# First mixer of a two-layer decoder trunk: 12 query projections in place of 16, rotary rows placed by transfers, and one reciprocal for two tiles

## The chip, the cores and the metric

The kernel runs on one core of one Trainium2 chip. The metric is the device time of one execution, in microseconds (us); a kernel's time is the median of several runs. The kernel before takes 1875.57 us (median of 3 runs, 1875.18 to 1875.59). Engines are named as in the profile: PE is the matmul engine and PEld its weight loads, DVE the vector engine, ACT the scalar engine, POOL the GpSimd engine, and SP the engine that issues most of the transfers.

## The reference

The input is 512 tokens of 1024 numbers. Two layers each do half a gated FFN, a token mixer, and half a gated FFN, all with residual sums and root-mean-square norms. The first layer's mixer is multi-head latent attention with 16 heads, the second layer's is a sparse attention. Only the first mixer's form is rewritten. It computes:

```python
proj = h @ w_in
c_q, c_kv, k_rope = proj[..., :384], proj[..., 384:640], proj[..., 640:]
q = (rmsnorm(c_q, q_norm) @ w_uq).reshape(B, S, 16, 64 + 32)
kv = (rmsnorm(c_kv, kv_norm) @ w_ukv).reshape(B, S, 16, 64 + 64)
q_nope, q_rope = q[..., :64], apply_rotary(q[..., 64:], cos, sin)   # 32 rotary numbers a head
k_rope = apply_rotary(k_rope, cos, sin)                             # one for all heads
s = (q_nope . k_nope + q_rope . k_rope) * 96 ** -0.5                # causal
p = softmax(s);  o = p @ v;  return o @ w_o
```

`apply_rotary` takes a vector's two halves x1, x2 and gives x1 cos - x2 sin, x1 sin + x2 cos.

## The kernel before

All products run in a form that splits each fp32 operand into a high part (a copy by ACT) and a low part (the difference, by DVE or POOL), and does three matmuls for each product: high by high, high by low, low by high (`mm3`, lines 166 to 168; `split`, line 170). Weights come by a transfer into a raw tile `wr` of two buffers, ACT copies the high part and DVE, or POOL while `lo_pool` is set, subtracts the low part (`wslab`, line 136).

The mixer (`mla`, line 664) holds everything transposed: a row is a feature, 512 tokens lie along it. It projects the input with six weight slabs of 128 features (`pc` and `pr` on PE, tiles of 128x512), three for the query latent `cqh`/`cql`, two for the key-value latent, and one for the rotary key. A head then has one query tile of 128 rows: 64 plain rows, 32 rotary rows and the same 32 rotary rows with their halves swapped. `query` (line 771) therefore does one projection for each head, 9 matmuls of 128x512 (three parts of the latent by three products), multiplies it on DVE by a table `cst` that has ones, cosines and sines, and splits it (high on ACT, low on POOL for all but the first two heads). The key tile of a head has 64 plain rows and 64 rotary rows, so that one score product adds plain and rotary parts. `keys` (line 762) projects two heads at a time, 6 matmuls, and splits each half of the result straight into the 64 rows of that head's key tile: two copies on ACT and two differences on DVE for a pair. `vals` (line 745) makes the values, half of the heads at a time.

The attention is a list of 64 tiles, 16 heads `h` by four query blocks `i` = 3, 2, 1, 0, with 512, 384, 256 and 128 keys (`attend`, line 591). `front` (line 781) does a tile's scores `s` on PE, the shift and row minimum on DVE (`softmax_tile`, line 657, shown as CUSTOM_DVE at line 661), the exponential with its row sum on ACT, a reciprocal of the sum on DVE (line 791) and the product with it on POOL (line 792). Four tiles later `probs_T` (line 611) transposes the tile on PE (`pt`), and ACT and DVE split it into `pth` and `ptl`. `end` (line 795) does the head's product with the values on PE (`o`, line 627). The scores have two banks, so PE cannot put a third tile of scores down before DVE has read the first of the three.

In between, where the order of the program has room, PE works on what later heads need: `query(h + 2)` at the start of each head, `keys` for a pair two heads ahead, the second half of the values, and from head 8 on parts of the output projection `po` (`w_o`, line 637). A scheduler puts the instructions of each engine into one fixed order; at run time each engine takes its own in that order and waits for semaphores of the others. SP takes its transfers in order too.

The sparse mixer uses the same `softmax_tile`, and one reciprocal for each branch of a tile (`probs` in `nsa`).

Of the kernel before, what the change touches and what calls it, by code (L numbers as in the profile page):

```python
# [55 lines left out]
NG = 3  # L56

# [7 lines left out]
class Kern:  # L65
# [13 lines left out]
    def setup(self):  # L79
# [8 lines left out]
        self.sts, self.nst = [small[:, 12 + 3 * i : 15 + 3 * i] for i in range(6)], 0  # L88
# [563 lines left out]
    def stat(self):  # L652

        self.nst += 1
        return self.sts[self.nst % 6]
# [8 lines left out]
    def mla(self, gain_next):  # L664
        nc, tc, a = self.nc, self.tc, self.a
        with ExitStack() as pools:
# [4 lines left out]
            cst = mp.tile([P, S], F32, name="cst")  # L671
            nc.scalar.dma_start(cst, a["c_rope"])
            mask = mp.tile([P, S], F32, name="mask")
# [3 lines left out]
            kh, kl = self.parts(self.four()), self.parts(self.four())  # L677
            ckvp, self.qt = self.parts(self.four()), self.parts(self.four())
# [10 lines left out]
            def rows(col):  # L689
                pb = self.norm_bcast(col)  # L690
                t = tp.tile([P, S], F32, tag="o", bufs=12, name="row")
                nc.scalar.activation(t, pb, AF.Copy)
                return t
# [21 lines left out]
            for k in range(2):  # L715
                c = tp.tile([P, S], F32, tag="o", bufs=12, name="c")
# [6 lines left out]
            p = self.proj(a["mla_w_in"][5], P, xh, xl, "pr")  # L723
            kr = tp.tile([P, S], F32, tag="o", bufs=12, name="kr")
            nc.vector.tensor_tensor(kr, p, row, op=ALU.mult)
            crot = tp.tile([P, S], F32, tag="p", bufs=6, name="crot")
            nc.scalar.dma_start(crot, a["c_krope"])
            nc.vector.tensor_tensor(kr, kr, crot, op=ALU.mult)
            kr2 = tp.tile([64, S], F32, tag="ot", bufs=1, name="kr2")
            nc.scalar.activation(kr2, kr[64:128, :], AF.Copy)  # L730
            krs = tp.tile([P, S], F32, tag="o", bufs=12, name="krs")
            nc.vector.tensor_tensor(krs[64:128, :], kr[0:64, :], kr2, op=ALU.add)
            up = slice(64, 128)
            self.split(krs[up, :], kh[0][up, :], kl[0][up, :])

            def rotary(i):
                nc.scalar.activation(kh[i][up, :], krs[up, :], AF.Copy)
                nc.gpsimd.tensor_scalar(kl[i][up, :], f32v(kl[0][up, :]), 1.0, 1.0, op0=ALU.mult, op1=ALU.mult)

            rotary(1)  # L740


            vt = [[None] * 4 for _ in range(4)]

# [23 lines left out]
            def query_slab(h):  # L768
                return self.wslab(a["mla_w_q"][h], (3, P), "act")

            def query(h, w=None):
                p = self.proj(None, P, cqh, cql, "pq", w or query_slab(h))
                t = tp.tile([P, S], F32, tag="tq", bufs=2, name="tq")
                nc.vector.tensor_tensor(t, p, cst, op=ALU.mult)
# [4 lines left out]
            qs, oh, ol, o32 = {}, [], [], [None]  # L779

            def front(h, i):
                if i == 3 and 2 < h + 2 < H:
                    qs[h + 2] = query(h + 2)
# [5 lines left out]
                st = self.stat()  # L789
                self.softmax_tile(s, mask[:, S - n : S], i, nq[:, i : i + 1], p_sb, st[:, 0:1], st[:, 1:2])  # L790
                nc.vector.reciprocal(st[:, 2:3], st[:, 1:2])
                nc.gpsimd.tensor_scalar(p_sb[:, :n], p_sb[:, :n], st[:, 2:3], 1.0, op0=ALU.mult, op1=ALU.mult)
                return p_sb, last

            def end(h):
                o = self.bank("o", "o")
                self.pv(o, pth[h % 2], ptl[h % 2], lambda j: vt[j][h // 4][:, h % 4, :], True, True)
                if h % 2 == 0:
                    o32[0] = tp.tile([P, S], F32, tag="o32", bufs=2, name="o32")
                self.o_out(o, o32[0], h % 2, tp)  # L800
                if h % 2 == 1:
                    hi = tp.tile([P, S], F32R, tag="o", bufs=12, name="oh")
                    lo = tp.tile([P, S], F32R, tag="o", bufs=12, name="ol")
# [6 lines left out]
                if h % 2 == 1 and h + 3 < H:  # L810
                    keys((h + 3) // 2)
                if h >= 8 and h % 2 == 0:
                    self.w_o(a["mla_w_o"][0], oh[:4], ol[:4], [h // 2 - 4], False)
# [7 lines left out]
            cq = self.norm_col(QL, sums[1], eps=eps)  # L821
            nc.vector.tensor_scalar(nq, cq, -MLA_SCALE, None, op0=ALU.mult)
            for i in range(2, 4):
# [535 lines left out]
```

## Time and profile before

| what | us |
|---|---|
| median of 3 runs | 1875.57 |
| the profiled execution, own time | 1875.46 |
| its span, first to last instruction | 1873.7 |
| PE busy in the span | 1852.1 |
| first mixer: projections (344 to 396) | 52 |
| first mixer: attention with what lies between (396 to 530) | 134 |
| first mixer: rest of the output projection (530 to 558) | 28 |
| sparse mixer's attention (1301 to 1510) | 209 |

Lines are those of the kernel before. An engine's busy time counts overlapping instructions once. Matmuls overlap, so a matmul of 389 ns does not cost PE 389 ns: what it costs is the distance from its start to the next one's. A wait is shown in square brackets behind an instruction, with the engine that ended it.

### The profile page before, as it was taken

The numbers are of one execution on the slowest core, as the hardware profiler recorded it, in microseconds if no ns is written. First come the engines' busy times: TensorE is split into PE (matmuls) and PEld (weight loads), VectorE is DVE, ScalarE is ACT, GpSimd is POOL, SyncE is SP. The second block draws the span as 40 slices with busy tenths as digits, with TensorE's granted clock in tenths as the row PEclk, the third lists the DMA queues.
The fourth block names the chain that finished last, engine by engine and source line by source line (L and its number), as shares of the span: only waits on it lengthen the run. The fifth ranks groups of instructions, "written<-read, shape, count | busy, mean of one in ns | idle before, by whom it ended". The sixth has DMA issues, their size and how long they took to land.

```text
span 1873.7 us, 32771 instructions
## 1 busy us (share of the span) xinstructions
PE 1852.1 (99%) x12460; PEld 1687.8 (90%) x12460; DVE 1546.0 (83%) x2920; ACT 1080.7 (58%) x2039; POOL 241.9 (13%) x331
## 2 busy tenths in 40 slices
PE   8999999999999999999999999999999999999998
PEld 8999999878889999998999999988888889999997
DVE  8988886588789988886998888665988989988885
ACT  8545554478766544554655454435887866454454
POOL 0000000046710000000000000014666500000000
PEclk9999999999999999999999999999999999999999
DMA  6333332111232333322333333223122133333321
GB/s 244 128 102 102 102 107 98 56 50 46 71 120 94 120 104 104 102 93 93 108 113 103 112 112 98 97 93 103 63 72 65 35 110 124 111 104 102 106 79 67
DMA packets 75902, 183.26 MB, mean 98 GB/s; under 512 B 9040, under 2 KB 37072, under 8 KB 75744
## 3 DMA queue, kind: packets, MB, share of 16 engines
q1 hardware_dynamic: 72800, 176.39, 28.7%
q10 hardware_dynamic: 2944, 4.77, 0.7%
q8 instruction: 98, 1.61, 0.3%
q14 instruction: 60, 0.49, 0.1%
HBM read 178.96 MB, written 2.16 MB: 97 GB/s over the span
## 4 chain that ended last, share of the span: by engine, by line
PE 51%; DVE 2%; ACT 0%; issue 0%; DMA 0%; POOL 0%; ACTq 0%; DVEq 0%; SPq 0%
PE pd L166 4%; PE pd L168 4%; PE pd L167 4%; PE px L361 3%; PE px L362 3%; PE px L363 3%; PE pg L361 2%; PE pg L363 2%; PE pg L362 2%; PE pq L362 2%; PE pq L361 2%; PE pq L363 2%; PE o L1163 2%; PE pt L1138 2%; PE pp L166 1%; PE pp L168 1%
## 5 line engine op out<-in xcount | busy, mean ns | idle before, releaser
L167 PE MATMUL pd<-al,wd 128*128 128x512 f32 x576 | 224.1, 389 | 0.0
L168 PE MATMUL pd<-ah,wd 128*128 128x512 f32 x576 | 224.0, 389 | 0.0
L166 PE MATMUL pd<-ah,wd 128*128 128x512 f32 x576 | 224.0, 389 | 0.0
L361 PE MATMUL px<-four,wh 128*128 128x256 f32 x632 | 175.3, 277 | 0.3 <-ACT pg L493 0.2
L362 PE MATMUL px<-four,wh 128*128 128x256 f32 x632 | 174.5, 276 | 0.0
L363 PE MATMUL px<-four,wl 128*128 128x256 f32 x632 | 174.5, 276 | 0.0
L362 PE MATMUL pq<-four,wh 128*128 128x256 f32 x632 | 174.5, 276 | 0.0
L363 PE MATMUL pq<-four,wl 128*128 128x256 f32 x632 | 174.4, 276 | 0.0
L361 PE MATMUL pq<-four,wh 128*128 128x256 f32 x632 | 174.4, 276 | 0.0
L174 ACT ACTIVATE wd<-wdr 128x384 fp32r<-128x384 f32 x192 | 99.3, 519 | 102.0 <-issue 76.9
L175 DVE TENSOR_TENSOR wl<-s,wh 128x512 fp32r<-128x512 f32 x79 | 54.5, 690 | 119.7 <-ACT wh L174 119.7
L413 DVE SCALAR_TENSOR_TENSOR h<-pd,h 128x512 f32<-128x512 f32 x216 | 147.5, 683 | 6.1 <-PE pd L168 6.1
L168 PEld LDWEIGHTS pd<-ah,wd 128*128 128x128 f32 x576 | 108.1, 188 | 22.5
L174 ACT ACTIVATE wh<-s 128x512 fp32r<-128x512 f32 x79 | 49.8, 630 | 134.5 <-PE px L362 128.8
L166 PEld LDWEIGHTS pd<-ah,wd 128*128 128x128 f32 x576 | 108.1, 188 | 19.5
L167 PEld LDWEIGHTS pd<-al,wd 128*128 128x128 f32 x576 | 108.0, 188 | 19.5
L147 ACT ACTIVATE w<-wr 128x1024 fp32r<-128x1024 f32 (+5 forms) x91 | 80.3, 890 | 75.0 <-PE po L168 17.5
L361 PEld LDWEIGHTS px<-four,wh 128*128 128x128 f32 x632 | 118.6, 188 | 1.2 <-ACT pg L493 0.9
L362 PEld LDWEIGHTS px<-four,wh 128*128 128x128 f32 x632 | 118.7, 188 | 0.0
L361 PEld LDWEIGHTS pq<-four,wh 128*128 128x128 f32 x632 | 118.6, 188 | 0.0
L363 PEld LDWEIGHTS px<-four,wl 128*128 128x128 f32 x632 | 118.6, 188 | 0.0
L362 PEld LDWEIGHTS pq<-four,wh 128*128 128x128 f32 x632 | 118.6, 188 | 0.0
(362 smaller groups left out, 6102.0 us busy)
## 6 DMA issues: line engine op xcount, KB each, us to landing
wr<-in_w_gu SPq DMA_DIRECT2D x93, 512.0 KB, 3.2
ru<-in_w_gu SPq DMA_DIRECT2D x79, 512.0 KB, 4.2
wdr<-in_w_down SPq DMA_DIRECT2D x192, 192.0 KB, 2.4
wdr<-in_w_down SPq DMA_DIRECT2D x24, 256.0 KB, 2.9
wr<-in_mla_w_o SPq DMA_DIRECT2D x8, 512.0 KB, 3.2
wr<-in_nsa_w_q SPq DMA_DIRECT2D x8, 512.0 KB, 3.2
th<-btab_d SPq DMA_DIRECT2D x16, 256.0 KB, 3.3
wr<-in_nsa_w_o SPq DMA_DIRECT2D x8, 512.0 KB, 3.4
```

What stands on the lines that cost most here:

```text
L147: self.copied = nc.scalar.activation(wh[:, m], raw[:, m], AF.Copy)
L166: mm(out, wh, xh, start=first, stop=False)
L167: mm(out, wh, xl, start=False, stop=False)
L168: return mm(out, wl, xh, start=False, stop=last)
L174: nc.scalar.activation(hi, src, AF.Copy)
L175: (nc.gpsimd if pool else nc.vector).tensor_tensor(lo, src, f32v(hi), op=ALU.subtract)
L361: mm(out, wh[:, p], xh, start=first and p == 0, stop=False, skip_group_check=True)
L362: mm(out, wh[:, p], xl, start=False, stop=False, skip_group_check=True)
L363: mm(out, wl[:, p], xh, start=False, stop=last and p == KP - 1, skip_group_check=True)
L413: nc.vector.scalar_tensor_tensor(self.h[c], p, 0.5, self.h[c], op0=ALU.mult, op1=ALU.add)
L1138: nc.tensor.transpose(pt[:, j * P : j * P + P], p_sb[:, j * P : j * P + P], self.ident)
L1163: mm(out, vs[g][:, j, br * P : (br + 1) * P], x, start=False, stop=last and t == 1 and j == 2 * z + 1, skip_group_check=True)
```

## The change

Queries. The weight columns are laid out anew: eight slabs hold the 64 plain columns of two heads each, and four slabs hold the 32 rotary columns of four heads each. `queries(pair)` does one projection for the plain rows of two heads, `turned(f)` one for the rotary rows of four heads. `turned` multiplies its result by two tables `rot` (cosines and sines) on DVE and splits both products into a tile `qr`. `queries` splits a pair's result in one operation on all 128 rows (ACT, then DVE) into a tile `wide`, and transfers, issued by SP, put the plain 64 rows and twice 32 rotary rows into each head's tile; only the first pair is split straight into place. Swapped halves are no longer projected for queries: the keys' rows for the sines are swapped instead (the order of `kr` in `mla_w_in` and the signs in `c_krope`).

Keys. `keys` also splits a pair in one operation into another `wide` tile and four transfers place it; only the first pair goes straight into place. The rotary rows of the other three key tiles are placed by six transfers instead of copies.

Order. The rotary key, the first rotary projection and the first pair of queries come ahead of the keys and values. `lo_pool` is set before the rotary key's projection, so the low parts of its weights and of those after it are made by POOL. An exponential of one column is put in the code ahead of the first values. `keys` is called in `front` and `w_o` at heads 10 to 13 (`OUT`) instead of behind heads 8, 10, 12 and 14.

Reciprocals. Two tiles of a head share one reciprocal of two columns, and POOL's two products come behind it. In the sparse mixer the two branches of a short tile share one.

```diff
+OUT = 10, 11, 12, 13
...
-            def query(h, w=None):
-                p = self.proj(None, P, cqh, cql, "pq", w or query_slab(h))
-                t = tp.tile([P, S], F32, tag="tq", bufs=2, name="tq")
-                nc.vector.tensor_tensor(t, p, cst, op=ALU.mult)
-                qh, ql = self.qtile(), self.qtile()
-                self.split(t, qh, ql, pool=h > 1)
-                return qh, ql
...
             def keys(pair, w=None):
                 p = self.proj(a["mla_w_k"][pair], P, ckvh, ckvl, "pk", w)
+                t = wide[0]
+                if pair:
+                    self.split(p, t[:, :S], t[:, S:])
                 for e in range(2):
-                    b = (2 * pair + e) % 4
-                    self.split(p[64 * e : 64 * e + 64, :], kh[b][0:64, :], kl[b][0:64, :])
+                    x, m = (2 * pair + e) % 4 * S, slice(64 * e, 64 * e + 64)
+                    if not pair:
+                        self.split(p[m, :], kh[e][m, :], kl[e][m, :])
+                        continue
+                    for z in range(2):
+                        nc.sync.dma_start(f32v(k4[z])[m, x : x + S], f32v(t)[m, z * S : z * S + S])
...
+            def turned(f, w=None):
+                p = self.proj(None, P, cqh, cql, "pq", w or query_slab(H // 2 + f))
+                for z in range(2):
+                    t = f32v(wide[1])[:, z * S : z * S + S]
+                    nc.vector.tensor_tensor(t, p, rot[z], op=ALU.mult)
+                    x = 2 * z * S
+                    self.split(t, qr[:, x : x + S], qr[:, x + S : x + 2 * S], pool=f > 0)
+            def queries(pair, w=None):
+                p = self.proj(None, P, cqh, cql, "pq", w or query_slab(pair))
+                t = wide[1]
+                if pair:
+                    self.split(p, t[:, :S], t[:, S:])
+                for e in range(2):
+                    q, m, o, j = sets[2 * (pair % 2) + e], slice(64 * e, 64 * e + 64), 64 - 64 * e, 32 * ((2 * pair + e) % 4)
+                    if pair:
+                        nc.sync.dma_start(f32v(q)[m, :], f32v(t)[m, :])
+                    else:
+                        self.split(p[m, :], q[m, :S], q[m, S:])
+                    for z in range(2):
+                        nc.sync.dma_start(f32v(q)[o + 32 * z : o + 32 * z + 32, :], f32v(qr)[j : j + 32, 2 * z * S : 2 * z * S + 2 * S])
...
             def front(h, i):
-                if i == 3 and 2 < h + 2 < H:
-                    qs[h + 2] = query(h + 2)
+                if i == 3 and h % 2 == 0 and h + 2 < H:
+                    queries(h // 2 + 1)
+                if i == 1 and h % 2 == 0 and 2 <= h < H - 2:
+                    keys(h // 2 + 1)
+                if i == 3 and h % 4 == 1 and h + 3 < H:
+                    turned((h + 3) // 4)
+                if i == 3 and h in OUT:
+                    self.w_o(a["mla_w_o"][0], oh[:4], ol[:4], [OUT.index(h)], False)
...
-                nc.vector.reciprocal(st[:, 2:3], st[:, 1:2])
-                nc.gpsimd.tensor_scalar(p_sb[:, :n], p_sb[:, :n], st[:, 2:3], 1.0, op0=ALU.mult, op1=ALU.mult)
+                some.append((p_sb[:, :n], st[:, 4 + x : 5 + x]))
+                if x % 2:
+                    nc.vector.reciprocal(st[:, 3 + x : 5 + x], st[:, 3 + x : 5 + x])
+                    for t, r in some:
+                        nc.gpsimd.tensor_scalar(t, t, r, 1.0, op0=ALU.mult, op1=ALU.mult)
+                    some.clear()
...
+            turned(0)
+            queries(0)
...
             for pair in range(2):
                 keys(pair, [t[:, pair] for t in w])
-            wv = self.wslab(a["mla_w_v"][0], (2, S))
-            wq = query_slab(0)
-            vals(0, wv)
...
-            for i in range(2, 4):
-                rotary(i)
-            for h in range(3):
-                qs[h] = query(h, wq if h == 0 else None)
+            nc.scalar.activation(self.tiny[:, 1:2], self.tiny[:, 0:1], AF.Exp)
+            vals(0)
```

In the changed kernel lines count one higher up to line 663 (line 166 before is line 167), and more behind it. Three places show how instructions move.

On PE, where the second head (head 1) begins, the kernel before has query projections between the scores `s` and the transposes `pt`:

```order
L166 MATMUL pq<-cqh_4264,w 128x512
L167 MATMUL pq<-cql_4265,w 128x512
L168 MATMUL pq<-cqh_4264,w 128x512
L166 MATMUL s<-four,q 128x512
L167 MATMUL s<-four,q 128x512
L168 MATMUL s<-four 128x512
L166 MATMUL s<-four,q 128x384
L167 MATMUL s<-four,q 128x384
L168 MATMUL s<-four 128x384
L166 MATMUL pq<-cqh_4159,w 128x512
L167 MATMUL pq<-cql_4160,w 128x512
L616 MATMUL pt<-ident,p 128x128 x4
```

On PE at the same place the changed kernel has:

```order
L169 MATMUL pq<-cqh_4270,w 128x512
L167 MATMUL s<-four 128x512
L168 MATMUL s<-four 128x512
L169 MATMUL s<-four 128x512
L167 MATMUL s<-four 128x384
L168 MATMUL s<-four 128x384
L169 MATMUL s<-four 128x384
L617 MATMUL pt<-ident,p 128x128 x7
L167 MATMUL s<-four 128x256
L168 MATMUL s<-four 128x256
L169 MATMUL s<-four 128x256
L617 MATMUL pt<-ident,p 128x128 x2
```

The projections between them are gone: this head, and the one after it, consist of scores, transposes and the product with the values alone.

On SP the kernel before has, from the second half of the values on, only weight loads (`wr<-in_...`):

```order
L144 DMA wr<-in_mla_w_v 128x1024
L144 DMA wr<-in_mla_w_q 128x384
L144 DMA wr<-in_mla_w_k 128x256
L144 DMA wr<-in_mla_w_q 128x384 x2
L144 DMA wr<-in_mla_w_k 128x256
L144 DMA wr<-in_mla_w_q 128x384 x2
```

On SP in the changed kernel the same loads stand behind transfers from `qr` and `wide` into the query tiles (`four`, `q_4037`) and key tiles (`four`):

```order
L145 DMA wr<-in_mla_w_v 128x1024
L788 DMA four<-qr 32x1024 x3
L784 DMA four<-wide_4039 64x1024 x2
L788 DMA four<-qr 32x1024
L145 DMA wr<-in_mla_w_k 128x256
L145 DMA wr<-in_mla_w_q 128x384
L788 DMA q_4037<-qr 32x1024 x3
L761 DMA four<-wide_4038 64x512 x4
L788 DMA q_4037<-qr 32x1024
L784 DMA q_4037<-wide_4039 64x1024 x2
L145 DMA wr<-in_mla_w_k 128x256
L145 DMA wr<-in_mla_w_q 128x384 x2
```

Each pair of heads now has ten transfers ahead of and between its weight loads, and some of them wait for heads that still read the tile they write.

On ACT, in the first FFN, far ahead of the mixer, the kernel before has the copies of the products:

```order
L477 ACTIVATE gains<-pg,gains 128x1 x2
L493 ACTIVATE pg<-px 128x256
L477 ACTIVATE gains<-pg,gains 128x1
L495 ACTIVATE uq<-pq 128x256
L497 ACTIVATE uq<-px 128x256
L174 ACTIVATE ah<-tu 128x512
```

On ACT at that place the changed kernel has:

```order
L494 ACTIVATE pg<-px 128x256
L478 ACTIVATE gains<-pg,gains 128x1
L858 ACT_TABLE_LOAD
L858 ACTIVATE gains<-gains 128x1
L496 ACTIVATE uq<-pq 128x256
L498 ACTIVATE uq<-px 128x256
L175 ACTIVATE ah<-tu 128x512
L501 ACTIVATE pg<-px 128x256
```

The exponential of one column depends on nothing in the mixer and has moved into the first FFN, with a load of its table; the FFN's own table is loaded again after eight more instructions, and the mixer's first exponential still has its own load.

More of the change, by code (lines that the diff above doesn't have):

```diff
@@ L87, in setup @@
         self.vtc, self.small_sums, self.stc = small[:, :12], small[:, 12:16], small[:, 32:]
-        self.sts, self.nst = [small[:, 12 + 3 * i : 15 + 3 * i] for i in range(6)], 0
+        self.sts, self.nst = [small[:, 12 + 4 * i : 16 + 4 * i] for i in range(5)], 0
         self.gains = cp.tile([P, 64], F32, name="gains")
@@ L670, in mla @@
             self.scr = tp, "p", 6
-            cst = mp.tile([P, S], F32, name="cst")
-            nc.scalar.dma_start(cst, a["c_rope"])
-            mask = mp.tile([P, S], F32, name="mask")
+            rot = [self.xp.tile([P, S], F32, tag="w2", bufs=2, name="rot"), mp.tile([P, S], F32, name="rot")]
+            for z in range(2):
+                nc.scalar.dma_start(rot[z], a["c_rope"][z])
+            qr = mp.tile([P, 4 * S], F32R, name="qr")
+            q2 = mp.tile([P, 4 * S], F32R, name="q2")
+            wide = [mp.tile([P, 2 * S], F32R, name=f"wide{z}") for z in range(2)]
+            mask = self.xp.tile([P, S], F32, tag="w2", bufs=2, name="mask")
             nc.scalar.dma_start(mask, a["c_mask"])
@@ L676, in mla @@
             ptl = [mp.tile([P, 3 * PTS + S], F32R, name=f"ptl{i}") for i in range(2)]
-            kh, kl = self.parts(self.four()), self.parts(self.four())
-            ckvp, self.qt = self.parts(self.four()), self.parts(self.four())
+            k4 = [self.four(), self.four()]
+            kh, kl = self.parts(k4[0]), self.parts(k4[1])
+            ckvp, q1 = self.parts(self.four()), self.four()
+            sets = [t[:, x * S : x * S + 2 * S] for t in (q1, q2) for x in (0, 2)]
             xh, xl = self.xh, self.xl
@@ L690, in rows @@
                 pb = self.norm_bcast(col)
-                t = tp.tile([P, S], F32, tag="o", bufs=12, name="row")
+                t = tp.tile([P, S], F32, tag="o", bufs=10, name="row")
                 nc.scalar.activation(t, pb, AF.Copy)
@@ L715, in mla @@
             for k in range(2):
[L716 removed]
+                c = tp.tile([P, S], F32, tag="o", bufs=10, name="c")
                 nc.vector.tensor_tensor(c, ps[k], rkv, op=ALU.mult)
@@ L721, in mla @@
                 ckvl.append(lo)
[L723 to L740, printed above, removed]
             vt = [[None] * 4 for _ in range(4)]
+            qs, oh, ol, o32, some = {}, [], [], [None], []
             def vals(half, w=None):
@@ new lines, in queries @@
+            def queries(pair, w=None):
[9 more added lines that the diff above has]
+                        self.split(p[m, :], q[m, :S], q[m, S:])
+                    for z in range(2):
+                        nc.sync.dma_start(f32v(q)[o + 32 * z : o + 32 * z + 32, :], f32v(qr)[j : j + 32, 2 * z * S : 2 * z * S + 2 * S])
+                    qs[2 * pair + e] = q[:, :S], q[:, S:]
@@ L1128, in front2 @@
                 p_sb = tp.tile([P, S], F32, tag="p", bufs=6, name="p")
-                for br in range(2):
-                    bs = slice(br * m, br * m + m)
-                    probs(h, br, i, sb[:, bs], p_sb[:, bs])
+                probs(h, (0, 1), i, sb, p_sb)
                 return p_sb, last
```

69 lines of the change are left out of this document (42 added, 27 removed).

## The prediction

> **What bounds the kernel now.** First the page's busy times:
>
> ```profile
> span 1873.7 us, 32771 instructions
> PE 1852.1 (99%) x12460; PEld 1687.8 (90%) x12460; DVE 1546.0 (83%) x2920; ACT 1080.7 (58%) x2039; POOL 241.9 (13%) x331
> ```
>
> PE is busy for 99% of the span. That is an average, so I read the stages next, by windows (stretch, its length, then busy time of PE, PEld, DVE, ACT, POOL):
>
> ```profile
> 344.00:396.00 52.00, 52.00 (x250) 43.50 (x250) 31.20 (x74) 23.98 (x43) 3.26 (x5) 1.00 0.19 60
> 396.00:530.00 134.00, 129.89 (x727) 110.07 (x726) 106.07 (x319) 104.72 (x271) 87.11 (x112) 1.00 0.18 58
> ...
> 396.40:411.40 15.00, 13.23 (x74) 10.57 (x73) 12.42 (x45) 13.02 (x32) 12.02 (x16) 1.00 0.20 62
> ...
> 520.10:527.90 7.80, 7.37 (x50) 6.31 (x48) 7.51 (x25) 6.75 (x18) 2.13 (x4) 1.00 0.20 67
> ...
> 1301.00:1510.00 209.00, 207.59 (x1192) 174.47 (x1190) 187.06 (x596) 172.88 (x436) 132.38 (x164) 1.00 0.19 62
> ```
>
> In the mixer's projections PE never waits. In its attention PE is idle for 4.1 of 134 us, of which 1.77 lie in the first 15 us. DVE is busy 79% there and ACT 78%. So a matmul taken out of this stage shortens the kernel by its slot, as long as PE stays the engine that is last. The stretch from 520.10 is the exception to learn from: the last two heads, with hardly any projection between their scores. There DVE is busy for 96% of the time, and PE waits for it.
>
> **What a slot is worth.** The time line of PE, first and last of 22 matmuls of 128x512 that follow each other:
>
> ```profile
> 515.11 0.39 PE L168 MATMUL po<-oh,w 128*128 128x512 f32 x1
> ...
> 519.87 0.39 PE L168 MATMUL po<-oh,w 128*128 128x512 f32 x1
> ```
>
> 21 distances in 4.76 us are 0.2267 us for one matmul of 128x512. The Trainium skill's page "TensorE: Matmul & The Clock Gate" (section "Wait — 56ns, not 53.3ns?") gives 215.7 ns from start to start at 512 columns; the trace has 226.7 at a granted clock of 1.00, so the measured one counts, and by the page's figure the first term below would be 7.8 us in place of 8.2.
>
> **Term 1, the projections.** What writes and reads `pq` in the mixer:
>
> ```profile
> L166 PE MATMUL pq<-cqh,w x48: 387/397/478, 390.2 to 504.1; 128*128 128x512 f32 x48
> ...
> L167 PE MATMUL pq<-cql,w x48: 387/391/397, 390.5 to 504.4; 128*128 128x512 f32 x48
> ...
> L168 PE MATMUL pq<-cqh,w x48: 388/393/478, 390.7 to 504.6; 128*128 128x512 f32 x48
> L774 DVE TENSOR_TENSOR tq<-pq,cst x16: 671/680/692, 393.0 to 505.0; 128x512 f32<-128x512 f32 x16
> ```
>
> 144 matmuls are 16 projections of 9. Twelve projections are 108. **36 x 0.2267 = 8.16 us less.** No other matmul is added or removed.
>
> **Term 2, the start of the attention.** PE's two longest waits there:
>
> ```profile
> 397.51 0.44 PE L166 MATMUL s<-four 128*128 128x384 f32 x1 [0.25 <-DVE tq L774]
> ...
> 400.24 0.39 PE L166 MATMUL s<-four 128*128 128x256 f32 x1 [1.01 <-DVE small L661]
> ```
>
> Scores wait because DVE still works on the norm's column and on the queries of heads 0 to 2. In the changed order the norm's column and the queries of heads 0 and 1 come ahead of the first values, whose 24 matmuls (5.4 us) cover them. All 1.77 us could go, or none if another wait takes the place; I take **1.3 us less**.
>
> **Term 3, heads without projections.** Fewer projections, done for two or four heads at once, leave heads with scores, transposes and values alone. By the order these are heads 1, 2, 4, 7, 13, 14 and 15, seven against two before (14 and 15). What such a head costs is seen in the stretch of 96% DVE, whose scores begin at:
>
> ```profile
> 520.09 0.28 PE L166 MATMUL s<-four 128*128 128x256 f32 x1
> ...
> 520.58 0.31 PE L166 MATMUL s<-four 128*128 128x128 f32 x1
> ...
> 521.44 0.50 PE L166 MATMUL s<-four 128*128 128x512 f32 x1 [0.19 <-DVE small L661]
> ...
> 523.33 0.44 PE L166 MATMUL s<-four 128*128 128x384 f32 x1
> ...
> 524.87 0.33 PE L166 MATMUL s<-four 128*128 128x256 f32 x1
> ...
> 525.73 0.22 PE L166 MATMUL s<-four 128*128 128x128 f32 x1
> ```
>
> These are 2 + 1 + 4 + 3 + 2 + 1 = 13 blocks of 128 keys, and a head has 10. PE is idle for 7.80 - 7.37 = 0.43 us, so 0.33 us a head. DVE's softmax step gives the upper end (mean 543 ns):
>
> ```profile
> L661 DVE CUSTOM_DVE_ANT_0 p<-s,mask,small 128x512 f32<-128x512 f32 (+1 forms) x64 | 34.0, 543 | 3.8 <-PE s L168 2.5 <-PE pt L616 0.4 <-POOL w L153 0.2
> ```
>
> If PE loses one more such step in each of these heads, it is 0.33 + 0.54 = 0.87 us. I take 0.5, nearer to the row that was seen: five more heads give **2.5 us more**, with ends of 1.6 and 4.4. What speaks against the upper end is that DVE itself gets less to do in the attention:
>
> ```profile
> L791 DVE RECIPROCAL small<-small 128x1 f32<-128x1 f32 x64 | 10.0, 158 | 6.3 <-ACT p L662 5.3
> L175 DVE TENSOR_TENSOR four<-pk,four 64x512 fp32r<-64x512 f32 x16 | 11.0, 687 | 3.4 <-ACT four L174 3.3
> ```
>
> 32 reciprocals go (5.1 us), key differences fall from 16 to 9 (4.8), products with the rotary table from 16 to 8 (5.4), and query differences on DVE rise from 2 to 11 (6.2): about 9 us less, all beside PE's work except in the bare heads. The shared reciprocal also makes a tile wait for its neighbour's exponential, some 0.6 us; the four tiles between scores and transposes hide it while POOL and DVE are not behind.
>
> **Term 4, transfers and weights.** No transfer within the chip is in the trace of before. The nearest are small loads (KB each, us to landing) and the issue of one on SP:
>
> ```profile
> wr<-in_mla_w_q SPq DMA_DIRECT2D x16, 192.0 KB, 2.3
> ...
> cb<-btab_d SPq DMA_DIRECT2D x16, 64.0 KB, 2.7
> ...
> wr<-in_mla_w_k SPq DMA_DIRECT2D x6, 128.0 KB, 2.0
> ...
> 402.38 0.33 SPq L144 DMA_DIRECT2D wr<-in_mla_w_k  x1
> ```
>
> The tightest place is the keys of heads 4 and 5. From the end of `pk` to the scores of head 4 it takes a copy on ACT (0.61 by the row of `four` under term 6), the difference on DVE (0.69), two issues (0.66) and a landing (2.0 to 2.7): 4.0 to 4.6 us. PE has between them one transpose, nine matmuls of `pq` (2.04) and eight of `o`:
>
> ```profile
> 505.52 0.60 PE L616 MATMUL pt<-ident,p 128*128 128x128 f32 x4
> 505.87 0.43 PE L166 MATMUL s<-four,q 128*128 128x384 f32 x1
> ...
> 506.73 0.84 PE L627 MATMUL o<-pth,vt 128*128 128x512 f32 x4
> 507.40 0.80 PE L627 MATMUL o<-ptl,vt 128*128 128x512 f32 x4
> 508.04 0.45 PE L166 MATMUL pk<-four,w 128*128 128x512 f32 x1
> ```
>
> From 506.73 to 508.04 the eight take 1.31 us, and four transposes 0.35. That is 1.31 + 2.04 + 0.1 = 3.5 us, so PE waits 0.5 to 1.1 us; I take 0.8, and 0.2 for the next pair, which has two projections between. The later pairs have an output slab or a bare head more. Then the weights: slabs now come in bunches, and SP must pass the transfers first; the groups by line (busy us, mean ns) and SP's own waits (us in total, times, longest):
>
> ```profile
> L153 POOL TENSOR_TENSOR w<-wr,w 128x384 fp32r<-128x384 f32 x12 | 12.5, 1045 | 7.3 <-ACT w L147 7.3
> L147 ACT ACTIVATE w<-wr 128x384 fp32r<-128x384 f32 x11 | 5.7, 515 | 4.3 <-PE po L168 3.6 <-POOL p L792 0.7
> ...
> SPq L144 <- POOL w L153: 54.5, 19, 7.2
> ```
>
> A query slab keeps one of the two raw buffers for 0.33 + 2.3 + 0.52 + 1.05 = 4.2 us, so two buffers give one slab in 2.1 us, and PE uses one up in 2.04. SP waits for POOL's low part for 54.5 us already, so loads start late today as well. In the bunch at heads 9 and 10 (keys, two query slabs, an output slab) I count 0.8 us, in the one at heads 5 and 6 0.4. **2.2 us more** in all, between 0 (all of it beside other work) and 5 (every one of these four places at 1.25).
>
> **Term 5, the sparse mixer.** 32 reciprocals of 128 go, 5.1 us of DVE; PE is idle there for only 209.00 - 207.59 = 1.4 us. I take **0.4 us less**, between 0 and 1.4.
>
> **Term 6, the exponential put ahead.** The order shows it in the first FFN, so the mixer's own load stays and two loads are added. A load's row:
>
> ```profile
> 399.64 0.61 ACT L174 ACTIVATE four<-tq 128x512 fp32r<-128x512 f32 x1
> 400.27 1.28 ACT L662 ACT_TABLE_LOAD   x1
> 401.57 0.72 ACT L662 ACTIVATE p<-p,small 128x512 f32<-128x512 f32 x1
> ```
>
> 1.28 us each, and the next exponential starts 1.30 after the load does. The first falls between the copy of one product and the end of the next (12 matmuls of half the columns, about 1.4 us), the second ahead of a gate on an engine that is busy 58%. I take nothing; without cover it is 2.6 us. The Trainium skill's page "ScalarE: Activation LUTs" (section "What ACT_TABLE_LOAD costs") counts 2.66 us for a switch, a drain of 1.38 with the load. The rows here show no such drain around the load; by the page two switches would keep ACT for 5.3 us.
>
> **The sum.** -8.2 - 1.3 + 2.5 + 2.2 - 0.4 = -5.2 us. The profiled execution took 1875.46 us, 0.1 below the median of the runs (1875.57): **1870.3 us.**
>
> **The rivals.** *Almost all of it is kept.* Terms 3 and 4 at their low ends, term 2 at 1.77: -8.16 - 1.77 + 1.6 + 0 - 0.4 = -8.7, 1866.7 us. For it: DVE and POOL (14 query differences fall to 6) get lighter. Against it: the 96% stretch.
> *It is given back.* Terms 3 and 4 at their high ends: -8.16 - 1.3 + 4.4 + 5 - 0.4 = -0.5, 1875 us. For it: SP's late loads and the bunches.
> *Slower: SP holds the weights behind the transfers.* If a pair's key slab is loaded only after the pair's query transfers, the way is copy 0.6, difference 0.7, six issues 2.0, load 0.33 + 2.0, and about 1.2 for ACT and POOL: 6.8 us from `pq` to `pk`. A bare head is 30 blocks of scores (1.7 us by term 1's slot), ten transposes (0.9) and the values (1.31), 3.9 us; with no more to do meanwhile PE loses 2.9 us, at all seven pairs 20, and with this in the place of term 4 the sum is +12.6, 1888 us. From 1.6 us a pair on it is slower by more than 0.2%. Against it: at most pairs the order has 24 matmuls of values or output between the two.
> *The table loads show.* If PE waits for both in the FFN, +2.6: 1872.9 us. It is the page's switch cost as a mechanism, priced by the row.
>
> **How the numbers follow.** Forecast 0.44, almost all kept 0.17, given back 0.22, table loads 0.05, slower 0.12. A change of 0.2% (3.75 us) is about what a measurement of this kernel can tell from none. Faster by more than that are the first two, 0.61; within it 0.27; slower 0.12. The range from 1865.0 to 1875.5 leaves out the slower case and the outer ends of the second and third, 0.2 together.
>
> **What would show it.** Term 1: `pq` with 36 matmuls on each of its lines. Term 2: less than 0.5 us idle before the first transposes. Term 3: waits of `s` for DVE (line 662 of the changed kernel) in heads 1, 2, 4, 7, 13 to 15, some 0.5 us each. Term 4: scores of head 4 that wait for a transfer, `pk` or `pq` that wait for POOL's low parts. Term 6: a gap on PE near 46 us. The forecast is wrong if PE's idle time in the attention leaves 5 to 11 us, or if the time goes elsewhere than into the mixer.

## The result, and the profile after

The changed kernel takes **1890.99 us** (median of 6 runs, 1887.34 to 1893.24), the kernel before 1875.44 (6 runs). The ratio is 1.0079, with a 95% interval from 1.0068 to 1.0090: slower by 15.6 us, where 5.2 us faster was forecast. The profiled execution took 1887.34 with a span of 1885.6 us, 11.9 more than before; the other five executions took 2.9 to 5.9 us longer at a mean granted clock of 0.995 to 0.997 in place of 0.998, and no trace shows where, so that the profile accounts for 11.9 of the 15.6 us. From the starts of PE's matmuls, that is +1.0 up to the first scores, **+11.5 from the first scores to the last output product** (161.3 to 172.8), +0.9 from there to the sparse attention, -1.2 from there to PE's last matmul and -0.3 behind it.

The page's first lines, then windows (stretch, its length, busy time of PE, PEld, DVE, ACT, POOL, granted clock, DMA share, GB/s): attention with the output projection, and the stretch of head 9:

```profile
span 1885.6 us, 32737 instructions
PE 1852.0 (98%) x12424; PEld 1681.6 (89%) x12424; DVE 1533.0 (81%) x2844; ACT 1075.7 (57%) x2029; POOL 235.1 (12%) x324
```

```profile
397.40:570.40 173.00, 156.51 (x813) 126.11 (x813) 115.64 (x305) 115.23 (x286) 74.51 (x101) 0.99 0.46 124
...
469.40:492.90 23.50, 18.40 (x85) 13.68 (x85) 9.50 (x26) 12.28 (x30) 13.99 (x17) 1.00 0.53 140
```

The same stretch of the kernel before, for comparison:

```profile
396.40:557.90 161.50, 157.39 (x850) 132.38 (x849) 127.03 (x350) 119.94 (x296) 88.00 (x113) 1.00 0.21 68
```

PE has 36 matmuls fewer, as the change says, but is idle for 173.0 - 156.5 = 16.5 us in place of 4.1. None of the other engines is near its limit: in the stretch of head 9 POOL, the busiest of them, is busy for 14.0 of 23.5 us and DVE for 9.5. So engines wait for each other. DMA's share went from 0.21 to 0.46. Issues of this part (KB each, median us to landing), then ACT's longest groups of waits (us in total, times, longest):

```profile
wr<-in_mla_w_o SPq DMA_DIRECT2D x8, 512.0 KB, 4.4
four<-wide SPq DMA_DIRECT2D x27, 128.0 KB, 2.4
q<-wide SPq DMA_DIRECT2D x8, 256.0 KB, 3.8
```

```profile
ACT w L148 <- DMA wr<-in_mla_w_o: 14.8, 5, 5.9
ACT pth L620 <- PE pt L617: 8.1, 11, 2.9
```

In the kernel before the same loads of output slabs landed sooner, and ACT's longest waits were for PE:

```profile
wr<-in_mla_w_o SPq DMA_DIRECT2D x8, 512.0 KB, 3.2
```

```profile
ACT w L147 <- PE po L168: 15.1, 6, 4.2
```

Busier DMA engines, weights that land late, ACT waiting for them: all of it points to the traffic of the transfers. The experiments show that this first reading was wrong in its main point.

### The profile page after: what moved, and what is told of

It reads as the page before. It is cut to its first block, busy times and chain, and to the rows that moved or that the text cites. A ratio compares the mean times of both kernels' runs of the same rounds, so it can differ in the third digit from the quotient of the medians.

```text
span 1885.6 us, 32737 instructions
## 1 busy us (share of the span) xinstructions
PE 1852.0 (98%) x12424; PEld 1681.6 (89%) x12424; DVE 1533.0 (81%) x2844; ACT 1075.7 (57%) x2029; POOL 235.1 (12%) x324
## 5 line engine op out<-in xcount | busy, mean ns | idle before, releaser
L362 PE MATMUL px<-four,wh 128*128 128x256 f32 x632 | 175.5, 278 | 0.7 <-ACT pg L494 0.7
L154 POOL TENSOR_TENSOR w<-wr,w 128x512 fp32r<-128x512 f32 (+2 forms) x63 | 77.3, 1245 | 451.2 <-ACT w L148 447.8
L362 PEld LDWEIGHTS pq<-four,wh 128*128 128x128 f32 x632 | 118.6, 188 | 0.0
L364 PEld LDWEIGHTS pq<-four,wl 128*128 128x128 f32 x632 | 118.6, 188 | 0.0
```

Source lines behind the costliest of these rows:

```text
L154: nc.gpsimd.tensor_tensor(wl[:, xs], raw[:, xs], f32v(wh[:, xs]), op=ALU.subtract)
L362: mm(out, wh[:, p], xh, start=first and p == 0, stop=False, skip_group_check=True)
L364: mm(out, wl[:, p], xh, start=False, stop=last and p == KP - 1, skip_group_check=True)
```

## The experiments

All are the changed kernel with one edit, unless said otherwise. "Stretch" is the distance on PE's time line from the first scores to the last output product. Ratios stand against runs of the kernel before on the same chip.

| run | median us | ratio [95%] | stretch |
|---|---|---|---|
| before | 1875.4 to 1877.3 | 1 | 161.3 |
| changed | 1890.99 | 1.0079 [1.0068, 1.0090] | 172.8 |
| e1 no moves | 1869.78 | 0.9966 [0.9955, 0.9978] | 156.2 |
| e2 one reciprocal a tile | 1894.65 | 1.0098 [1.0082, 1.0113] | 175.2 |
| e3 keys and queries direct | 1872.63 | 0.9981 [0.9971, 0.9990] | 157.3 |
| e4 ACT's queue | 1909.33 | 1.0176 [1.0161, 1.0191] | 194.9 |
| e5 half the bytes | 1873.58 | 0.9984 [0.9975, 0.9993] | 155.7 |
| e6 keys direct | 1873.80 | 0.9985 [0.9975, 0.9994] | 155.4 |
| e7 queries direct | 1875.09 | 0.9989 [0.9979, 0.9998] | 157.5 |
| e8 rows unread | 1890.16 | 1.0070 [1.0053, 1.0087] | 175.5 |
| e9 weights ahead | 1882.79 | 1.0034 [1.0021, 1.0047] | 165.5 |
| e10 before, 36 matmuls fewer | 1866.87 | 0.9944 [0.9929, 0.9959] | 153.3 |
| e11 keys direct, weights ahead | 1874.36 | 0.9987 [0.9977, 0.9996] | 157.2 |
| e12 keys direct, no early exponential | 1874.93 | 0.9987 [0.9977, 0.9996] | 155.7 |
| e13 order held, half the bytes | 1889.49 | 1.0065 [1.0049, 1.0081] | 171.3 |
| e14 order of e5, all bytes | 1875.03 | 0.9990 [0.9981, 1.0000] | 157.5 |
| e15 keys direct, one reciprocal a tile | 1874.64 | 0.9988 [0.9978, 0.9997] | 156.7 |
| e16 before, shared reciprocals | 1876.88 | 0.9994 [0.9985, 1.0004] | 160.8 |
| e17 SP's order alone | 1894.24 | 1.0089 [1.0072, 1.0106] | 177.6 |
| e18 three raw buffers | 1887.21 | 1.0054 [1.0037, 1.0071] | 170.6 |

### First: is it the transfers, and which?

e1, without the transfers of later pairs:

```diff
-                    for z in range(2):
+                    for z in range(2 if pair < 2 else 0):
                         nc.sync.dma_start(f32v(k4[z])[m, x : x + S], ...)
...
```

> Leaves out: the on-chip transfers of query and key rows from pair 2 on (heads 4 to 15 use stale rows, so the numbers computed for them mean nothing); the splits into the wide tiles, the turned tiles and all matmuls stay. Theory A (the transfers: they hold SP's queue, crowd the DMA engines and make weights and queries late): the loss of 15.6 us goes and the gain that was forecast shows, 1868 to 1874. Theory B (the heads without projections are bound by DVE's chain and its shared reciprocal, with matmul gaps that then halve the clock): the transfers cost nothing, 1887 to 1893. In between, 1877 to 1884, both.

e2:

```diff
-                if x % 2:
-                    nc.vector.reciprocal(st[:, 3 + x : 5 + x], st[:, 3 + x : 5 + x])
+                if True:
+                    nc.vector.reciprocal(st[:, 4 + x : 5 + x], st[:, 4 + x : 5 + x])
```

> The first mixer takes a reciprocal for each tile again, directly behind its exponential; all else is the change's. Theory B1 (the shared reciprocal makes the first tile of a pair wait for the second, and so the transposes late): 1878 to 1885. Theory A (transfers): no gain, 1890 to 1893, perhaps 1 us more for 32 further instructions of 0.16 us on DVE.

e3 (e6 has its first half alone, e7 its second):

```diff
-                    self.split(p, t[:, :S], t[:, S:])
...
+                    self.split(p[m, :], kh[b][m, :], kl[b][m, :])
...
+                    self.split(p[m, :], q[m, :S], q[m, S:])
```

> Keys and query rows without position are split out of PSUM straight into their places, in halves of 64 partitions, for every pair (28 + 14 transfers less of some 74; the rotary rows still go by transfer); it costs about 13 more copies on ACT and 13 more subtractions on DVE of 0.4 to 0.7 us each. Theory A with the share by bytes (the keys and queries left out are some 60% of the bytes moved): 1880 to 1884. Theory A2 (SP's waits for the late turned rows hold the queue; these stay): 1886 to 1890. Theory B: 1891 to 1896, since DVE and ACT get more work.

e4, with `nc.scalar.dma_start` for `nc.sync.dma_start` in the three lines of `keys` and `queries`:

> The same transfers, issued from ACT's queue in place of SP's, so that no weight load stands behind them; ACT pays their issue. Theory A2 (what hurts is the order on SP, weights held behind transfers that wait): 1876 to 1885, less what ACT loses. Theory A1 (what hurts is the traffic itself on the DMA engines): 1889 to 1893. Theory B: 1891 or more, since ACT now waits for the low parts of POOL and DVE in the middle of its exponentials, up to 1905.

Without the transfers (e1) the kernel takes 1869.78 us, 0.5 us below the forecast for the change. The shared reciprocals are not the cause: undone, they gain nothing, and put alone into the kernel before (e16) they make no difference that can be told. Issued by ACT the transfers cost 18 us more; e4 lies above, and e3 below, every range set for it. In e3 DVE and ACT do more work (123.9 and 122.3 us busy in the stretch, by its windows, against 115.6 and 115.2), and yet the time is below that of the kernel before.

### Second: bytes, late rows, or late weights?

e5:

```diff
+                n = 2 * S if pair < 2 else S
...
-                        nc.sync.dma_start(f32v(q)[m, :], f32v(t)[m, :])
+                        nc.sync.dma_start(f32v(q)[m, :n], f32v(t)[m, :n])
```

> Leaves out: the second half of the columns of every on-chip transfer from pair 2 on (the rest of the rows is stale); number, order and waits of the transfers stay. With all of them left out the kernel took 1869.8, with all of them 1891. Theory A1 (what costs is the traffic, by bytes): about half of the 21 us comes back, 1879 to 1882. Theory A2 (what costs is that SP's queue stands at a transfer until its rows are ready, and the weights behind it come late): 1886 to 1891, for the rows are ready no earlier. Theory A3 (the scores wait for the transferred rows themselves, 2.3 to 3.8 us after issue): a transfer gets shorter by 0.5 to 1 us, 1884 to 1888.

> Only the keys are split straight into their places (24 transfers less, of 128 KB each); queries and rotary rows go by transfer as in the change. Keys and queries both direct took 1872.6. If the loss goes with the bytes (keys 3.1 MB of the 4.7 MB that both are): 1877 to 1880. If the keys are what comes late to the scores (they are made at the third tile of the even head, two heads ahead, and their transfers stand behind those of the queries): 1874 to 1877. If the queries are: 1885 to 1889.

> Only the query rows without position are split straight into their places (14 transfers less, of 256 KB each by the rows they write); keys and rotary rows go by transfer. By bytes: 1885 to 1888. If SP is held longest by the transfers that wait for the wide query tile, which stands one pair ahead of every use: 1878 to 1883. If the keys are what costs: 1887 to 1890.

e8:

```diff
-                qh, ql = qs[h]
+                qh, ql = qs[h] if h < 4 else (cqh[0], cql[0])
+                k1, k2 = (kh[h], kl[h]) if h < 4 else (ckvh[0], ckvl[0])
...
```

> All transfers are made as in the change, but from head 4 on the scores are multiplied out of the latents, which stand still (so the output means nothing): nobody waits for a transferred row any more, and no transfer waits for a score. Traffic and the order on SP stay. Theory A1 or A2 (traffic, or weights held on SP): 1883 to 1890. Theory A3 (the scores wait for the transferred rows): 1869 to 1874.

e9:

```diff
-        nc.sync.dma_start(dst, src)
+        with self.tc.high_priority(120) if self.lo_pool else nullcontext():
+            nc.sync.dma_start(dst, src)
```

> All transfers stay, in number, bytes and rows; only the weight loads of the two mixers, while POOL makes the low parts, are put 120 places earlier into SP's order, as far as a raw buffer is free, so that they stand between the transfers and not in bunches behind a pair's transfers. The bytes moved do not change. Theory A2 (SP's order: weights stand behind transfers that wait for their rows, with both raw buffers free): 1870 to 1877. Theory A1 (traffic by bytes crowds the DMA engines): 1887 to 1892.

e8 loses as much as the change although no score waits for a transferred row. The other four fit no theory (e6 misses its second range by 0.2 us). Half the bytes gave back everything, and so did the keys alone *and* the queries alone, which cannot each be the whole. What these runs share, e1 to e4 and e8 too, is that the scheduler, which counts with the length of a transfer, laid out all engines anew. In e8 the new order has bunches of its own: heads 10 and 13 take 6.4 and 5.0 us over their matmuls' slots. Weights ahead, with all bytes, gave back half, also with a new order everywhere.

### Third: the order held, the bytes changed

e13 and e14 separate the two. Edges of order between neighbours on each engine, without waits, hold all 1838 instructions of the mixer at the places of another kernel:

```diff
+    for x, y in zip(at, at[1:]):
+        x, y = v[f"I-{x}"], v[f"I-{y}"]
+        if x.engine == y.engine:
+            tc.add_manual_dep(y, x.name, info, reason="pinned")
```

> Leaves out: the second half of the columns of every on-chip transfer from pair 2 on, as in the run that took 1873.6. But the order of every engine's instructions in the mixer is held at that of the changed kernel, instruction by instruction (edges of order alone, no waits); the run with halves had let the scheduler lay out another order. If the order is what costs (weights bunched behind transfers on SP): 1885 to 1890, since half the bytes shorten only the landings. If the bytes cost: 1872 to 1878.

> The counterpart: the changed kernel with all its transfers at full length and the right output, but with every engine's order in the mixer held at the one that the scheduler laid out for the halved transfers. If the order is what costs: 1873 to 1878, a correct kernel that loses nothing against the one before. If the bytes cost: 1885 to 1892. The sum of the two theories' shares over this run and its counterpart should give the 17 us between the two kernels measured.

Windows of the stretch, of e13 and then of e14, and ACT's longest waits in e13 and then in e14:

```profile
400.70:572.30 171.60, 156.04 (x814) 126.47 (x814) 115.57 (x305) 115.10 (x286) 74.48 (x101) 0.99 0.35 97
```

```profile
400.60:558.30 157.70, 150.97 (x813) 126.72 (x812) 115.66 (x304) 114.04 (x286) 74.59 (x101) 0.99 0.51 134
```

```profile
ACT w L176 <- DMA wr<-in_mla_w_o: 12.8, 5, 5.8
```

```profile
ACT w L175 <- PE po L196: 19.6, 7, 4.0
ACT pth L647 <- PE pt L644: 5.1, 8, 1.6
```

**It is the order.** e13, with a DMA share of 0.35, stays at 171.6 us; e14, with every byte and a share of 0.51, takes 157.7. By the ratios the order is worth 1.0079 - 0.9990 = 0.89%, 16.7 us, with all bytes, and 1.0065 - 0.9984 = 0.81% with half of them (e13, e5). Halving the bytes is worth 1.0079 - 1.0065 = 0.14% in the one order and 0.9990 - 0.9984 = 0.06% in the other; the intervals leave room for some 0.3%, about a third of the loss. In e13 ACT still waits for output slabs, with half the bytes; in e14 its longest waits at the weights' copies are for PE, as in the kernel before: it has the slabs early.

What differs is seen on PE. The order from the third tile of head 9 to the end of head 10, each tile with the number of its matmuls in a row, of the changed kernel and of e14:

```
changed: s3 pt2 s3 pt o5 pk6 pq9 pq9 po12 po12 s3 pt4 s3 pt3 o3 pk6 s3 pt2 s3 pt po12 po12
e14:     s3 pt2 s3 pt pq9 po12 po12 s3 pt4 s3 pt3 o8 pk6 s3 pt2 s3 pt po12 po12
```

The changed kernel has four weight slabs in one bunch (keys, two of queries, one of output; the expectation of e18 below counts one too many) after a stretch with few projections; in e14 each of the heads 4 to 12 has its share. PE in the bunch waits for the four to come through SP, ACT and POOL:

```profile
478.24 0.39 PE L169 MATMUL pk<-four,w 128*128 128x512 f32 x1
478.47 0.39 PE L167 MATMUL pq<-cqh,w 128*128 128x512 f32 x1
...
482.73 0.39 PE L169 MATMUL pq<-cqh,w 128*128 128x512 f32 x1
484.19 0.50 PE L167 MATMUL po<-oh,w 128*128 128x512 f32 x1 [1.07 <-ACT w L148]
...
485.56 0.50 PE L169 MATMUL po<-oh,w 128*128 128x512 f32 x1 [0.64 <-POOL w L154]
...
487.72 0.39 PE L169 MATMUL po<-oh,w 128*128 128x512 f32 x1
490.01 0.50 PE L167 MATMUL po<-oh,w 128*128 128x512 f32 x1 [1.90 <-DVE wide L176]
```

And what it waited for, on SP, ACT, POOL and DVE:

```profile
478.39 0.33 SPq L145 DMA_DIRECT2D wr<-in_mla_w_o  x1
```

```profile
483.08 1.06 ACT L148 ACTIVATE w<-wr 128x1024 fp32r<-128x1024 f32 x1 [2.99 <-DMA wr<-in_mla_w_o]
484.04 1.14 ACT L175 ACTIVATE qr<-wide 128x512 fp32r<-128x512 f32 x2
488.04 0.60 ACT L175 ACTIVATE wide<-pq 128x512 fp32r<-128x512 f32 x1 [2.86 <-POOL qr L176]
```

```profile
476.65 1.72 POOL L154 TENSOR_TENSOR w<-wr,w 128x256 fp32r<-128x256 f32 x2
...
484.21 2.55 POOL L154 TENSOR_TENSOR w<-wr,w 128x512 fp32r<-128x512 f32 x2 [3.01 <-DMA four<-wide]
486.71 2.52 POOL L176 TENSOR_TENSOR qr<-wide,qr 128x512 fp32r<-128x512 f32 x2
```

```profile
480.71 1.29 DVE L771 TENSOR_TENSOR wide<-pq,rot 128x512 f32<-128x512 f32 x2 [0.72 <-PE pq L169]
489.26 0.69 DVE L176 TENSOR_TENSOR wide<-pq,wide 128x512 fp32r<-128x512 f32 x1 [7.26 <-POOL qr L176]
489.87 0.68 DVE L649 TENSOR_TENSOR h<-po,h 128x512 f32<-128x512 f32 x1
```

Read from the top: the first row of POOL holds the low parts of the keys' slab and of a query slab; the second of them ends at 478.37 and frees a raw buffer, and 0.02 us later SP issues the output slab. It lands by 483.08, and ACT has stood still for 2.99 us with it at the head of its queue. Then POOL makes its low part (2.55 us), and only behind that the low parts of the turned rows (2.52), which read the tile `wide`. Until the first of them is done ACT may not write the queries' high part into that tile (2.86), and until the second is, DVE not their low part (7.26). DVE's subtraction ends at 489.95 and with it the last reading of the bank of `pq`; PE's next output product starts at 490.01. So PE loses 1.07, 0.64 and 1.90 us to one slab, 3.6 of the 7.3 us that head 9 takes more than in the kernel before; 1.2 us are waits of `o` for DVE ahead of the bunch, and the rest, small delays behind each wait, is not split up here. Four engines, each taking its queue in order, hold each other up through one raw buffer and one `wide` tile. That this chain is what the order costs at this place is read from the trace; the tile alone was not doubled.

e17 and e18 try the parts of that chain by themselves, with PE, DVE, ACT and POOL held at the changed kernel's order:

> The changed kernel with all transfers at full length; PE, DVE, ACT and POOL are held at the changed kernel's order, instruction by instruction. On SP alone the weight loads of the attention are moved up to where, in the changed kernel's trace, the raw buffer they write had come free (7 loads by 5 to 22 us, the others by less or nothing); the transfers keep their order among themselves. Theory S (weights stand behind transfers on SP, and that alone is the loss): 1875 to 1880. Theory P (the order of the engines that work, with projections and weights' copies put close to their use, is as much to blame, since most raw buffers came free late by ACT's and POOL's own order): 1881 to 1887. If SP's order hardly matters: 1888 to 1891.

```diff
-        raw = self.wp.tile([P, 1024], F32, tag="wr", bufs=2, name="wr")
+        raw = self.wp.tile([P, 1024], F32, tag="wr", bufs=3, name="wr")
```

> Leaves out: the high part of the query latent (its low part stands in its place, which frees the space). A third raw weight buffer, in the whole kernel; in the mixer PE, DVE, ACT and POOL are held at the changed kernel's order, and SP's weight loads are moved up to where the third buffer would have come free. The FFNs are laid out anew with three buffers, so the mixer's stretch is compared by itself: 172.8 us from the first scores to the last output product in the changed kernel, 161.3 before; the worst head (head 9, whose projections and output slabs need five weight slabs in a row) takes 8.4 us over its matmuls' slots. If the bunches starve because two raw buffers hand on one slab at a time: head 9 at 2 to 4 us, the stretch 160 to 167. If ACT's and POOL's own order keeps the slabs late whatever the buffers: head 9 at 7 to 10 and the stretch 170 to 178.

SP's issue of the output slab in e17, whose head 9 begins at 474.49:

```profile
483.44 0.33 SPq L173 DMA_DIRECT2D wr<-in_mla_w_o  x1
```

The stretch of head 9 in e17, in e18, and where e14 has its head 9:

```profile
474.50:500.00 25.50, 19.74 (x85) 14.81 (x85) 9.45 (x26) 12.01 (x30) 15.11 (x17) 0.93 0.49 136
```

```profile
474.10:495.60 21.50, 18.95 (x84) 15.06 (x84) 9.46 (x26) 12.01 (x30) 15.15 (x17) 0.92 0.54 141
```

```profile
471.40:483.20 11.80, 11.80 (x65) 10.17 (x64) 7.43 (x20) 7.70 (x19) 11.12 (x14) 1.00 0.69 175
```

SP's order alone is not the cause: with the weights put ahead of the transfers nothing comes back. At 1894.24 us e17 lies above all three of its ranges. In it the output slab is issued 8.95 us after the head begins, just as in the changed kernel (478.39 - 469.44): not the transfers but the raw buffer held it. The 4.8 us that its stretch is longer lie in heads 0 to 3 and 9, in which its granted clock fell to half four times (0.96 over the stretch), where the changed kernel's did once (0.99). A third buffer takes head 9 from 23.5 to 21.5 us, 6.4 over its slots and between the two ranges set for it, and the stretch from 172.8 to 170.6, at the near end of its second range. Its granted clock was 0.92 in head 9 where the changed kernel's was 1.00, which by itself can have cost 0.08 x 21.5 = 1.7 us at most; so the buffer gives back some 2 to 3.6 of the 7.3 us in head 9. That leaves most of the loss to the orders of PE, ACT, POOL and DVE among themselves, with projections bunched. This is what remains, not what a run shows: which of the four engines' orders would give back most stays open, since no run exchanges one of them alone. e14 has no such bunch there: its head 9, with 33 matmuls of queries and output in it (48 with keys in the changed kernel), keeps PE busy for all of 11.80 us, with DMA at 0.69.

### Fourth: the parts by themselves

e10 is the kernel before with `cqh[:n], cql[:n]`, n = 2, in the projections of 12 heads. e11, e12 and e15 are e6 with the edit of e9, without the early exponential, and with the edit of e2. e16 is the kernel before with the changed reciprocals of both mixers.

> The kernel before, with the last third of the query projection left out in 12 of 16 heads: 36 matmuls of 128x512 fewer on PE and nothing else changed on any other engine (the queries of these heads miss a third of the latent). If term 1 of the prediction is priced right (0.2267 us for each where PE is the bound) 1867 to 1868.5. If DVE and ACT take over as the bound when PE has less to do: 1869 to 1873.

> Keys direct, as in the run that took 1873.8, with the weight loads also put ahead. If some of the loss by late weights is still in that kernel: 1869 to 1872. If it has none left and its idle time is that of heads without projections: 1873 to 1875.

> Keys direct, without the exponential that stands in the first FFN, so without the two table loads there. If they lie beside PE's work, as term 6 took it: no change from 1873.8, within 1 us. If PE waits for them: 1871 to 1872.5.

> Keys direct (1873.8) with a reciprocal for each tile in the first mixer. In the changed kernel one for each tile made it 3.7 us slower, among weights that came late. If a shared reciprocal is worth 32 x 0.16 us on DVE in the bare heads alone, 1874.3 to 1876. If its wait for the second tile costs as much as it saves: 1873 to 1874.3. If it holds the transposes up: 1870 to 1873.

> The kernel before with only the shared reciprocals of both mixers. Term 5 and the remark under term 3 of the prediction: DVE gets 10 us less, beside PE's work; 0.4 us from the sparse mixer and up to 0.5 from the first: 1876 to 1877 where the kernel before takes 1876.8 (its median in the last two calls), so no difference that can be told. If POOL's products come late by the neighbour's exponential: 1878 to 1880.

Fewer matmuls alone are worth about what they should be: 8.2 us by the spans of the two profiles (1865.5 against 1873.7), 10.2 us by the medians on one chip, with an interval of 7.7 to 13.3. Once the order is a good one, weights ahead, the exponential and the reciprocals make no difference that these runs can tell; e11 came out in its second range. The lowest ratio of a correct kernel is that of e3, 0.9981 [0.9971, 0.9990], below the kernel before; the intervals of e6, e7, e11, e12, e14 and e15 overlap with it.

## Why the prediction was wrong

PE's time in each head, from its first scores to the next head's, less the slots of the matmuls in it (columns times 0.2267 / 512), for heads 0 to 14:

| heads | before | changed | e14 |
|---|---|---|---|
| 1, 2, 4, 7, 13, 14 (without projections by term 3) | 8.53 | 14.62 | 12.41 |
| 3, 5, 6, 8, 9, 10, 12 (term 4) | 8.95 | 23.91 | 10.94 |
| 0, 11 | 2.96 | 1.52 | 1.50 |

**Term 1 was right.** `pq` has 36 matmuls on each of its lines, and e10 gives 8.2 us by its span for 36 fewer (10.2 by its median, with 8.2 inside the interval).

**Term 2 came true at its place and was given back behind it.** The trace counts 0.4 us of waiting on PE before the first transposes, less than the 0.5 foretold, and head 0 takes 1.4 us less over its slots (0.60 in place of 2.03). Heads 1 and 2 take 2.8 more (in the first row above), and what lies ahead of the first scores takes 1.0 more, which no term had.

**Term 3 was right in kind and too small.** It measured 14.62 - 8.53 = 6.1 us where 2.5 was taken, above its upper end of 4.4. The waits of `s` for DVE are where it put them (1.49 us in head 2, 0.68 in head 7, 1.97 in head 13), but uneven, not some 0.5 in each head. In e14 the same heads cost 3.9 more; two of them, 4 and 7, have projections there.

**Term 4 is the step that failed**, and in it the weights, not the rows: the scores of head 4, for which 0.8 us was taken, begin without a wait, and no wait of PE in these heads is for a transferred row. "In the bunch at heads 9 and 10 (keys, two query slabs, an output slab) I count 0.8 us, in the one at heads 5 and 6 0.4." The whole term was 2.2, at most 5. It measured 23.91 - 8.95 = 15.0 us, half of it in head 9 alone (8.35 against 1.02 before and 0.91 in e14). Another 5.4 us lie in head 3, where values, keys and two query projections come together; that bunch was not priced at all. The other two had been seen in the order and were priced as a rate: so many us a raw buffer is held, over two buffers. The 4.2 us taken for that are a query slab's; the output slab in the bunch of head 9 held its buffer from 478.39 to 486.76, 8.4 us. And a rate counts each slab by itself. It leaves out what is queued behind a late slab on ACT and POOL, the tile `wide` that one pair's rows and the next pair's share, and that DVE stands behind both. In e14, without the bunch at head 9, the term measures 10.94 - 8.95 = 2.0. That this is close to the 2.2 taken is luck: head 3 costs 4.0 more there too, and the six other heads together 2.0 less than before.

6.1 + 15.0 - 1.4 - 8.2 for the slots of term 1 makes the stretch 11.5 us longer, as measured. PE's idle time, 16.5 us, is above the 5 to 11 that the prediction named as its bounds.

**Term 5** cannot be told from nothing: e16 is 0.9994 [0.9985, 1.0004], and the -1.2 us from the sparse attention on is not seen in all kernels that share this code. **Term 6 was right**: the load is at 45.4 us, PE's wait there is 0.2 us as before, and e12 gains nothing.

The slower rival came near in time, 1888 us, and had the wrong mechanism: it put the cost on SP's queue, key slabs behind query transfers, and e17 takes that away without gain. Its price was also by pairs, where the loss is in a few bunches.

## What to carry to other kernels

Where a scheduler orders instructions by its own estimate of durations, an edit moves work that it never touches; hold the order and change the one thing, or take the other's order and keep the thing, before a time is put down to it. A bunch of work that needs weights is not priced by the rate of the buffers alone: follow one late item through every in-order queue, write down what stands behind it on each, and look for a tile that two of them share. And a kernel whose matmuls got fewer can be slower while no engine is busier.

## What the runs showed of the hardware

The granted clock fell to half for 3.4 us in stretches with much waiting, though PE was not idle for long at a time. From 413.16 to 416.56 us of the changed kernel it is 0.50 (0.79 from 412 to 420), and matmuls of 128x512 start 0.43 us apart; ahead of it, between 409.0 and 413.2, PE was busy for 2.56 of 4.20 us, and its longest wait was 1.49 us. PE's time line, then the windows:

```profile
413.83 0.63 PE L168 MATMUL s<-four,q 128*128 128x512 f32 x1
414.26 0.63 PE L169 MATMUL s<-four,q 128*128 128x512 f32 x1
414.69 0.63 PE L167 MATMUL pq<-cqh,w 128*128 128x512 f32 x1
...
416.81 0.40 PE L167 MATMUL pq<-cqh,w 128*128 128x512 f32 x1
417.05 0.39 PE L168 MATMUL pq<-cql,w 128*128 128x512 f32 x1
```

```profile
413.16:416.56 3.40, 3.07 (x8) 2.08 (x8) 1.72 (x10) 2.60 (x10) 3.29 (x5) 0.50 0.18 39
...
412.00:420.00 8.00, 7.20 (x27) 5.16 (x27) 3.73 (x15) 5.53 (x15) 7.81 (x9) 0.79 0.23 49
...
409.00:413.20 4.20, 2.56 (x17) 1.86 (x15) 4.20 (x13) 3.42 (x9) 1.11 (x1) 0.99 0.00 0
```

The Trainium skill's page "TensorE: Matmul & The Clock Gate" (section "Wait — 56ns, not 53.3ns?") gives 426.7 ns from start to start at 512 columns on the halved clock; the 0.43 here agrees. Head 9, with longer waits, kept a clock of 1.00 in this execution and had 0.92 at the same order in e13. What such a stretch costs depends on what PE has to do in it: head 3 takes 21.70 us with it and 21.71 in e13, at the same order, without. A transfer from tile to tile of 128 KB landed in 2.4 to 3.0 us (medians of three groups in the stretch), one of 256 KB in 3.4 to 3.8; 2.0 to 2.7 had been estimated from smaller loads.
